# Seven products instead of eight for two column blocks of the gating's v, in a two-layer hybrid decoder step

## Chip, cores and metric

The kernel runs on one core of a Trainium2 chip. The metric is the device time of one execution in microseconds (us); less is better. All arithmetic is 32-bit floating point; the large matmuls run in the replicated form fp32r, in which each operand is split into a high and a low part and three of the four part products are added (high x high, high x low, low x high).

## What is computed

A trunk of two layers is run for a prompt of 1024 positions and for 64 sample rows (8 sequences of 8), with shared weights and model width 1024. Layer 0 mixes positions by windowed attention, layer 1 by a gating MLP; each is followed by a convolutional feed-forward block. The change lies in the gating of layer 1:

```python
def sgu_mix(h, w_in, b_in, ln_g, ln_b, w_sp, b_sp, w_out):
    z = jax.nn.gelu(h @ w_in + b_in)
    u, v = jnp.split(z, 2, axis=-1)          # 2048 columns each
    v = layernorm(v, ln_g, ln_b)
    ...
    mixed = jnp.einsum('gts,bnsgc->bntgc', wm, vb) + b_sp[:, :tc].T[None, None, :, :, None]
    out = (u * mixed.reshape(B, T, D_SGU)) @ w_out
    return out, v
```

Here h is the normed input (1088 rows of 1024). The layer norm of v runs over all 2048 columns, so v is computed first; the spatial mixing runs over chunks of 128 positions.

## The kernel before

Most matrix products of the kernel go by a scheme of seven products (Strassen's in Winograd's form): rows, inner dimension and columns are each halved, and seven products of sums of the blocks replace eight products of the blocks. The function `pair` (L1659) does it for two tiles of 128 output columns at a time, with weights made by `pair_weights` (L1612), and sums of the blocks of h made by the norm (`Norm7.sums`, L1369, and `Norm7.split`, L1382, which splits them into high and low parts `th` and `tl`). The u half of the gating already goes this way.

The v half does not. It is computed with positions on the partitions: the stationary operand is a 128x128 block of h (transposed, high or low part), the moving operand is a row block of weights, 128x512. The loop over `n` (L1977) takes four blocks of 512 columns. For each there are nine row tiles: eight of the prompt (24 matmuls each: 8 inner blocks x 3 part products) and one of the samples, which has high and low parts side by side in one tile of 128 (`norm.pair`) and so takes 16. That makes 208 matmuls of 512 columns a block. The last three tiles of a block are done inner block by inner block (VLAST), so that the four weight buffers come free one after the other. Each tile is then finished: VectorE adds the bias (L2016), ScalarE applies GELU (L2019), VectorE takes statistics for the layer norm (L2020), and a DMA on ScalarE's queue writes the tile to a scratch in memory (L2022), from where it is later read column by column for the mixing (`sgu_load`).

Around this, in the order of the program:
- During n=0 the norm that precedes the stage is finished (`norm.finish`, L1405 and `apply`): VectorE and ScalarE write the second half of the columns of the operands `ha` and `hb`.
- During n=0, after the fourth tile, the spatial weights are loaded on SP's queue (`load_spatial`, L1948), and after the ninth tile masked on GpSimd and summed by one matmul (`prep_spatial`, L1961).
- During n=1 to n=3, after every second tile, GpSimd makes one of eight sums of blocks of h (`norm.sums`), and ScalarE and VectorE split it, all for the u half behind.
- At the end of n=3 the first weights for u are prepared, then `ln_stats` closes the layer norm's statistics, and the u loop begins.

Weights come in one stream (`Stream`, class at L262) of units of 128x1024, in the order of `plan()`, loaded on SP's queue into two raw buffers; `split` casts the high part on ScalarE and subtracts for the low part on VectorE, into a pool of eight weight buffers. Working tiles come from one pool of 37 slots of 128x1106 (NSLOT, L28); PSUM has eight banks. The order of instructions on each engine in this part is chosen by the compiler's list scheduler: by place in the program (moved up by `high_priority`) and by when, by its own model, operands and buffers are ready; at run time each engine takes its queue in that order.

Of the kernel before, what the change touches and what calls it, by code (L numbers as in the profile page):

```python
# [10 lines left out]
F32 = mybir.dt.float32  # L11
# [15 lines left out]
SG_BLOCKS = [4, 4, 4, 4]  # L27
NSLOT = 37  # L28
VLAST = 3
FRA, FRB = 1, 2  # L30
CHF = ((0, 416), (416, 416), (832, 256))
FIN = ((0, 2, 1), (2, 4, 0), (4, 6, 1), (6, 8, 0))
# [35 lines left out]
def plan():  # L68

    u = []  # L70
    for e in START:
        if e[0] == "A":
            u += [(("adaq", e[1], e[2]), 1024)]
        elif e[0] == "S":
            u += [(("ada", 0, SH1, e[1]), 1024)]
        elif e[0] == "W":
            u += [(("qkv", 2, e[1]), 1024)]
    for n in (0, 1):
        u += [(("qkv", n, kp), 1024) for kp in range(4)]
# [24 lines left out]
    for n in range(4):  # L104
        u += [(("sguv", n, kp), 1024) for kp in range(4)]
    for j in range(0, NS, 2):
        u += [(("ua", 2, j), 1024), (("ub", 2, j), 1024)]
    u += down("w_sgu_out", SG_BLOCKS)
    u += ffn(1)
    return u  # L110


def lay_weights(inp):
# [30 lines left out]
    for key, _ in plan():  # L144
# [3 lines left out]
        elif k == "adaq":  # L148
            a = ada[0][key[2] * 512:key[2] * 512 + 512, 1024 + key[1] * 256:1280 + key[1] * 256]
            a = a.reshape(4, 128, 256).transpose(1, 0, 2)  # L150
        elif k == "qkv":
            a = kpair(wq, key[1], key[2])
        elif k == "sguv":
            a = kpair(sin[:, DSGU:], key[1], key[2])
        elif k == "up":
# [105 lines left out]
class Stream:  # L261
# [11 lines left out]
    def dma(s):  # L273
# [15 lines left out]
    def split(s):  # L289
# [48 lines left out]
HP = 200  # L338


def build(nc, tc, a, ctx):
# [941 lines left out]
    class Norm7:  # L1283
# [82 lines left out]

            return s.ab[k][h][:, part, :]

        def sums(s, z, q, e):  # L1369

            zc = slice(z * 272, z * 272 + 272)
            a0, a1, b0, b1 = (s.ab[2 * q + b][h][:, :, zc].bitcast(F32) for b in range(2) for h in range(2))
            t = slot([128, 4, 272], name="T")
            for i, (p, m) in enumerate(((a1, a0), (b1, a1))):
                e.tensor_sub(t[:, 2:4, :], p, m)
                e.tensor_add(t[:, i, :], t[:, 2, :], t[:, 3, :])
            for i, (p, m) in ((2, (b1, 0)), (3, (b0, 2))):
                e.tensor_sub(t[:, i, :], p[:, 0, :], t[:, m, :])
                e.tensor_add(t[:, i, :], t[:, i, :], p[:, 1, :])
            s.tt[z, q] = t  # L1380

        def split(s, z, q):  # L1382
            t = s.tt.pop((z, q))
            s.th[z, q], s.tl[z, q] = slot([128, 4, 272], F32R, name="th"), slot([128, 4, 272], F32R, name="tl")
            A.copy(s.th[z, q], t)
            V.tensor_sub(s.tl[z, q], t, s.th[z, q].bitcast(F32))

        def rhs(s, i, z, q, part):

            if i < 4:  # L1390
                k, h = ((2 * q, 0), (2 * q + 1, 0), (2 * q + 1, 1))[i - 1]
                return s.half(k, h, part)[:, z * 272:z * 272 + 272]
            return (s.tl if part else s.th)[z, q][:, {5: 0, 7: 1, 6: 2, 4: 3}[i], :]

        def drop(s, what):

# [578 lines left out]
    todo = [(z, q) for z in range(2) for q in range(4)]  # L1975
    taken = []
    for n in range(4):  # L1977
        bv = slot([128, 512], name="bv")
        SP.dma_start(bv, a["bv"][0:1, n * 512:n * 512 + 512].broadcast_to([128, 512]))
        ws.ahead(4)  # L1980
        un = [ws.take("sguv") for _ in range(4)]
        ps = {}
# [16 lines left out]
        for i, t in enumerate((0, 1, 4, 5, 2, 3, 6, 7, 8)):  # L1999
            M = 128 if t < 8 else 64  # L2000
            if i <= 9 - VLAST:
                for kp in range(4):
                    for t_ in ((t,) if i < 9 - VLAST else (2, 3, 6, 7, 8)[5 - VLAST:]):
                        v_mm(t_, kp)
                    if i == 9 - VLAST:
                        un[kp] = None
                        if n < 3:
                            with tc.high_priority(offset=HP):
                                ws.split()
                        elif kp == 0:  # L2010
                            gen = pair_weights()
                            W = next(gen)
                        else:
                            next(gen)
            v = slot([128, 512], name="v")
            V.tensor_add(v[:M], ps[t][:M], bv[:M])  # L2016
            if M == 64:
                V.tensor_add(v[:M], ps[t][64:128], v[:M])
            A.activation(v[:M], v[:M], AF.Gelu_apprx_tanh)  # L2019
            V.bn_stats(stats[:M, t, n, :], v[:M])  # L2020
            if t < 8:
                A.dma_start(vscr[n, :, :, t, :], v.rearrange("p (j c) -> p j c", c=128))  # L2022
            else:
                A.dma_start(vscs[:, n * 512:n * 512 + 512], v[:64])
# [17 lines left out]
    del norm.pair  # L2042
    for k in range(0, 8, 2):
        norm.ab[k][1] = None
    for _ in range(4):
        next(gen)
    for t in range(9):
        ln_stats(t)

# [113 lines left out]
```

## Time and profile before

| what | value |
|---|---|
| median of 3 runs | 2590.87 us (2586.61 to 2592.92) |
| profiled execution, its own time | 2589.49 us |
| its span, first to last instruction | 2587.7 us |
| mean granted TensorE clock | 0.994 |
| HBM read, written | 228.06 MB, 63.07 MB |

The names of the engines in the profile: PE is TensorE's matmul, PEld its weight load, DVE is VectorE, ACT is ScalarE, POOL is GpSimd, SP is SyncE, whose queue issues the loads. L375 is the helper through which every matmul goes, so matmuls are told apart by the tile that they write: `v` in the stage that is changed, `m` in the pairs of seven products, `acc` and `misc` elsewhere. A row of a group has: line, engine, operation, output<-inputs, shapes, count | busy us, mean ns of one | idle us of the engine before them, and who ended it. A row of a stretch has, for each engine, busy us and the number of instructions.

### The profile page before, as it was taken

How to read it: one execution, taken by the hardware profiler on the slowest of the kernel's cores; microseconds unless marked ns; L12 is line 12 of the kernel's file. 1: busy time of each engine (PE TensorE's matmuls, PEld its weight loads, DVE VectorE, ACT ScalarE, POOL GpSimd, SP SyncE). 2: the span in 40 equal slices, each digit the busy share in tenths (PEclk: the TensorE clock that was granted, in tenths of full speed). 3: DMA queues.
4: the chain of work that ended last, by engine and by line, in shares of the span. 5: the costliest groups of instructions: out<-in, count | busy, mean ns of one | idle time of the engine just before them, and what ended most of it. 6: DMA issues, size and time to landing. Idle time of an engine off the chain costs nothing.

```text
span 2587.7 us, 45783 instructions
## 1 busy us (share of the span) xinstructions
PE 2535.6 (98%) x17916; PEld 2373.8 (92%) x17916; DVE 1616.8 (62%) x3254; ACT 982.6 (38%) x1939; POOL 1240.9 (48%) x1392
## 2 busy tenths in 40 slices
PE   7999999999999999999999999999999999999998
PEld 4667789999999999999788999999999999999998
DVE  5416866767767764456744555655687766676545
ACT  3216854533334331114325655212553333332203
POOL 2325631399999900001643755212179999940003
PEclk9999999999999999999999999999999999999999
DMA  8342214022222275453322534522112222254211
GB/s 302 102 153 100 74 57 139 10 80 81 85 81 76 93 288 181 159 187 127 91 84 76 169 127 156 200 99 74 66 59 76 76 80 79 77 192 158 89 45 70
DMA packets 113943, 292.20 MB, mean 113 GB/s; under 512 B 15328, under 2 KB 47136, under 8 KB 113696
## 3 DMA queue, kind: packets, MB, share of 16 engines
q1 hardware_dynamic: 82016, 232.49, 27.4%
q10 hardware_dynamic: 31712, 56.79, 5.8%
q8 instruction: 142, 2.33, 0.4%
q14 instruction: 73, 0.60, 0.1%
HBM read 228.06 MB, written 63.07 MB: 113 GB/s over the span
## 4 chain that ended last, share of the span: by engine, by line
PE 86%; DVE 6%; ACT 3%; POOL 2%; DMA 2%; issue 1%; SPq 0%; ACTq 0%; DVEq 0%; POOLq 0%
PE m L375 32%; PE acc L375 23%; PE misc L375 9%; PE v L375 7%; PE y L375 5%; PE u L375 5%; PE adaps L375 1%; POOL w L1622 1%; DMA raw<-wts 1%; ACT P L841 1%; PE rs L375 1%; DVE cv L1823 1%; PE pv L375 1%; DVE cv L1810 1%; PE sc L375 1%
## 5 line engine op out<-in xcount | busy, mean ns | idle before, releaser
L375 PE MATMUL m<-th,w 128*128 128x272 f32 x2944 | 562.6, 288 | 6.4 <-DVE ext L1676 6.3
L375 PEld LDWEIGHTS m<-th,w 128*128 128x128 f32 x2944 | 466.2, 188 | 7.0 <-issue 6.6
L375 PE MATMUL m<-tl,w 128*128 128x272 f32 x1472 | 424.9, 289 | 0.0
L536 DVE SCALAR_TENSOR_TENSOR x<-acc,mod,x 128x384 f32<-128x384 f32 (+1 forms) x312 | 159.6, 567 | 237.6 <-PE acc L375 232.0
L375 PE MATMUL m<-hb,w 128*128 128x272 f32 x2208 | 294.3, 289 | 0.0
L375 PEld LDWEIGHTS m<-hb,w 128*128 128x128 f32 x2208 | 285.1, 190 | 0.0
L375 PEld LDWEIGHTS m<-tl,w 128*128 128x128 f32 x1472 | 277.5, 189 | 0.0
L375 PE MATMUL acc<-gh,whi 128*128 128x384 f32 (+1 forms) x1152 | 255.9, 330 | 1.1 <-DVE mixed L2089 0.8
L375 PE MATMUL acc<-gl,whi 128*128 128x384 f32 (+1 forms) x1152 | 253.6, 328 | 0.6 <-DVE gl L1729 0.6
L375 PE MATMUL acc<-gh,wlo 128*128 128x384 f32 (+1 forms) x1152 | 253.2, 327 | 0.0
L309 ACT CAST whi<-raw 128x1024 fp32r<-128x1024 f32 (+1 forms) x108 | 109.7, 1017 | 377.9 <-PE acc L375 230.5
L1622 POOL TENSOR_TENSOR w<-raw,w 128x512 fp32r<-128x512 f32 x138 | 194.5, 1422 | 82.2 <-ACT w L1621 76.0
L375 PEld LDWEIGHTS acc<-gh,whi 128*128 128x128 f32 x1152 | 194.7, 188 | 10.2 <-issue 6.2
L375 PEld LDWEIGHTS acc<-gl,whi 128*128 128x128 f32 x1152 | 195.6, 188 | 0.9 <-DVE gl L1729 0.9
L1808 DVE SCALAR_TENSOR_TENSOR cv<-ext,cst,cv 128x1104 f32<-128x1104 f32 x88 | 125.4, 1460 | 112.9 <-ACT cv L1807 53.9
L375 PEld LDWEIGHTS acc<-gh,wlo 128*128 128x128 f32 x1152 | 195.7, 188 | 0.0
L1621 ACT CAST w<-Sa 128x512 fp32r<-128x512 f32 x92 | 56.8, 622 | 307.9 <-POOL Sa L1632 162.0
L1676 DVE TENSOR_TENSOR ext<-ev,m 128x272 f32<-128x272 f32 (+1 forms) x456 | 137.5, 338 | 47.6 <-PE m L375 39.3
L1303 POOL TENSOR_TENSOR nsq<-nsq 128x544 f32<-128x544 f32 x18 | 24.9, 1385 | 273.4 <-ACT nsq L1296 273.4
L1810 DVE SCALAR_TENSOR_TENSOR cv<-ext,cst,cv 128x1104 f32<-128x1104 f32 x88 | 155.6, 1802 | 0.1
L375 PE MATMUL m<-ha,w 128*128 128x272 f32 x1104 | 146.6, 289 | 0.0
L375 PEld LDWEIGHTS m<-ha,w 128*128 128x128 f32 x1104 | 141.2, 188 | 0.6
(293 smaller groups left out, 5506.8 us busy)
## 6 DMA issues: line engine op xcount, KB each, us to landing
raw<-wts SPq DMA_DIRECT2D x238, 512.0 KB, 4.0
wada<-wts SPq DMA_DIRECT2D x54, 512.0 KB, 4.3
pscr<-cv ACTq DMA_DIRECT2D x44, 544.0 KB, 5.5
p<-pscr SPq DMA_DIRECT2D x40, 544.0 KB, 5.5
xscr<-x ACTq DMA_DIRECT2D x24, 512.0 KB, 2.8
x<-xscr SPq DMA_DIRECT2D x24, 512.0 KB, 8.3
sscr<-mixed ACTq DMA_DIRECT2D x16, 544.0 KB, 3.5
vscr<-v ACTq DMA_DIRECT2D x32, 256.0 KB, 2.6
```

What stands on the lines that cost most here:

```text
L309: nc.scalar.copy(hi[:, :c], r[:, :c])
L375: PE.matmul(out, lhsT=l, rhs=r, start=start, stop=stop)
L536: V.scalar_tensor_tensor(xv, p[:, 0:w], gp, xv, op0=ALU.mult, op1=ALU.add)
L841: A.activation(p, p, AF.Exp, bias=nm[:, h:h + 1], scale=0.125, accum_out=su[:, h:h + 1])
L1303: (V if z or m == 7 else G).tensor_add(s.ss[z], s.ss[z], q)
L1621: A.copy(t[:, 0:512], src)
L1622: eng.tensor_sub(t[:, 512:1024], src, t[:, 0:512].bitcast(F32))
L1676: V.tensor_add(o, f(p), f(q))
L1808: V.scalar_tensor_tensor(t[:, 0:1104], e[:, 1:1105], cw(jj * 3 + 1), t[:, 0:1104], op0=ALU.mult, op1=ALU.add)
L1810: V.scalar_tensor_tensor(t[:, 0:1104], e[:, 0:1104], cw(jj * 3), t[:, 0:1104], op0=ALU.mult, op1=ALU.add)
L1823: V.tensor_mul(tg[:, 0:SEQ], tg[:, 0:SEQ], tu[:, 0:SEQ])
```

## The change

Blocks n=0 and n=1 stay as they are. Blocks n=2 and n=3 (`VW`) go by seven products. The rows are halved into positions 0 to 511 and 512 to 1023, the inner dimension by the parity of its 128-blocks, and the 512 columns into two of 256. The stationary operands are the block sums of h which the u half needs anyway; they are now made over all 544 columns of a half at once (four of them, in tiles of twice the length) and during n=0 and n=1, one of them on VectorE. The weight sums for v are new: `v_weights` makes eight pairs of high and low tiles, with GpSimd for sums and low parts. Each product has two halves z of two row tiles, in one bank of 2 x 256 columns, and VectorE adds the products up on the way out. The sample rows do not take the scheme: they use four plain quarters of the weights, of which one (index 0) serves only them. The spatial weights are loaded and prepared behind the last block.

The stream's units of these blocks are now quarters of 256 columns; every second one is loaded into a slot instead of a raw buffer. The core of the diff (`v_done` is the old finishing of a tile as a function; the sums over 544 columns and the changed indices of the u half are left out):

```diff
@@ plan(), dma(), split()
-        u += [(("sguv", n, kp), 1024) for kp in range(4)]
+        u += [(("vq" if n in VW else "sguv", n, kp), 1024) for kp in range(4)]
...
-        if i < s.NFIRST or (key[0] == "ada" and key[1] == 0 and key[2] != G2):
+        if i < s.NFIRST or key[0] == "vq" and key[2] % 2 or (key[0] == "ada" and key[1] == 0 and key[2] != G2):
             t = s.first()
...
-        if key[0] in ("ada", "adaq", "ua", "ub"):
+        if key[0] in ("ada", "adaq", "ua", "ub", "vq"):
...
+    def v_weights():
+        W = {}
+        def parts(i, src):
+            W[i] = [wp.tile([128, 1024], F32R, name="v7", tag="w") for _ in range(2)]
+            A.copy(W[i][0], src)
+            G.tensor_sub(W[i][1], src, W[i][0].bitcast(F32))
+        yield W
+        r11 = ws.take("vq")[1]
+        parts(1, r11)
+        yield
+        r12 = ws.take("vq")[1]
+        parts(2, r12)
+        yield
+        r22 = ws.take("vq")[1]
+        parts(4, r22)
+        yield
+        r21 = ws.take("vq")[1]
+        parts(0, r21)
+        G.tensor_add(r22, r21, r22)
+        yield
+        G.tensor_sub(r21, r11, r21)
+        G.tensor_sub(r11, r22, r11)
+        parts(6, r11)
+        yield
+        G.tensor_sub(r12, r12, r11)
+        parts(5, r22)
+        yield
+        parts(7, r21)
+        yield
+        parts(3, r12)
+        yield
+
+    def v_pair(n, W, bv, prep):
+        ev, bk, vt = {}, {}, {}
+        sps = bank("v")
+        def mul(i, z):
+            p = bk[i, z] = bank("v").rearrange("p (g c) -> p g c", c=256)
+            for g_ in range(2):
+                c = slice((2 * z + g_) * 128, (2 * z + g_) * 128 + 128)
+                m = 0
+                for q in range(4):
+                    for xl, wl in ((0, 0), (0, 1), (1, 0)):
+                        mm(p[:, g_, :], norm.cols(i, q, xl)[:, c], W[i][wl][:, q * 256:q * 256 + 256], m == 0, m == 11)
+                        m += 1
+            return p
+        def sample(i):
+            f, b = ((1, 0), (0, 0), (0, 1), None, (1, 1))[i]
+            for q in range(4):
+                for wl in range(2):
+                    mm(sps[:, f * 256:f * 256 + 256], norm.pair[:, 2 * q + b, :], W[i][wl][:, q * 256:q * 256 + 256],
+                       i in (1, 4) and q + wl == 0, i in (2, 0) and q + wl == 4)
...
+        for i in (1, 2, 4, 6, 5, 7, 3):
+            if i == 1:
+                e0 = slot([128, 2, 2, 256], name="ve")
+                e1 = slot([128, 2, 2, 256], name="ve")
+            for z in range(2):
+                p = mul(i, z)
+                a = e0[:, z]
+                if i == 1:
+                    V.tensor_add(a, p, wide(bv[:, 0:256]))
+                elif i == 2:
+                    V.tensor_add(out(0, 0, z), a, p)
+                elif i == 6:
+                    V.tensor_add(a, a, p)
+                elif i == 5:
+                    V.tensor_add(e1[:, z], a, p)
+                    V.tensor_add(a, a, wide(bv[:, 512:768]))
+                elif i == 7:
+                    V.tensor_add(a, a, p)
+                    V.tensor_add(out(1, 0, z), a, bk.pop((4, z)))
+                    done(0, z)
+                    V.tensor_add(out(1, 1, z), a, bk.pop((5, z)))
+                elif i == 3:
+                    V.tensor_add(out(0, 1, z), e1[:, z], p)
+                    done(1, z)
...
+            if i in (1, 2, 4):
+                sample(i)
+            W.pop(i)
+            prep()
+            if i == 4:
+                sample(0)
+                W.pop(0)
...
@@ the loop over n, now n = 0 and 1 only
-            if n == 0 and i == 3:
-                wsp, wbd, rb, tri = load_spatial()
-            if n == 0 and i == 8:
-                prep_spatial(wsp, wbd, rb, tri)
-                del tri
-            if n and i % 2 == 1:
-                while taken:
-                    norm.split(*taken.pop(0))
-                if todo:
-                    norm.sums(*todo[0], G)
-                    taken.append(todo.pop(0))
+            if n == 0 and i == 7:
+                norm.sums(0, G)
+            if n == 1 and i in (1, 3, 5):
+                norm.split(i // 2)
+                norm.sums(i // 2 + 1, V if i == 1 else G)
...
+    norm.split(3)
+    for n in VW:
+        bv = load_bias(n)
...
+        v_pair(n, W, bv, prep)
...
     for _ in range(4):
         next(gen)
+    wsp, wbd, rb, tri = load_spatial()
+    prep_spatial(wsp, wbd, rb, tri)
```

`done(h, z)` applies GELU to two row tiles at once and then finishes each as before. `prep` makes the next pair of weight tiles, of this block or of the one behind it.

More of the change, by code (lines that the diff above doesn't have):

```diff
@@ L29 @@
 VLAST = 3
+VW = (2, 3)
 FRA, FRB = 1, 2
@@ L1367, in half, with sums, split, cols @@
             return s.ab[k][h][:, part, :]
[L1369 to L1373, printed above, removed]
+        def sums(s, q, e):
+            a0, a1, b0, b1 = (s.ab[2 * q + b][h].bitcast(F32) for b in range(2) for h in range(2))
+            t, t2 = s.tt[q] = [slot([128, 2, 544], name="T") for _ in range(2)]
             for i, (p, m) in enumerate(((a1, a0), (b1, a1))):
[L1375 to L1388, printed above, removed]
+                e.tensor_sub(t2, p, m)
+                e.tensor_add(t[:, i, :], t2[:, 0, :], t2[:, 1, :])
+            for i, p, m in ((0, b1, t), (1, b0, t2)):
+                e.tensor_sub(t2[:, i, :], p[:, 0, :], m[:, 0, :])
+                e.tensor_add(t2[:, i, :], t2[:, i, :], p[:, 1, :])
+        def split(s, q):
+            for j, t in enumerate(s.tt.pop(q)):
+                hi = s.th[q, j] = slot([128, 2, 544], F32R, name="th")
+                lo = s.tl[q, j] = slot([128, 2, 544], F32R, name="tl")
+                A.copy(hi, t)
+                V.tensor_sub(lo, t, hi.bitcast(F32))
+        def cols(s, i, q, part):
             if i < 4:
                 k, h = ((2 * q, 0), (2 * q + 1, 0), (2 * q + 1, 1))[i - 1]
-                return s.half(k, h, part)[:, z * 272:z * 272 + 272]
-            return (s.tl if part else s.th)[z, q][:, {5: 0, 7: 1, 6: 2, 4: 3}[i], :]
+                return s.half(k, h, part)
+            j = {5: 0, 7: 1, 6: 2, 4: 3}[i]
+            return (s.tl if part else s.th)[q, j // 2][:, j % 2, :]
+        def rhs(s, i, z, q, part):
+            return s.cols(i, q, part)[:, z * 272:z * 272 + 272]
         def drop(s, what):
@@ L1973, in ln_stats, with v_done @@
         V.scalar_tensor_tensor(mv[:M, t, 0:1], mv[:M, t, 0:1], -1.0, mv[:M, t, 1:2], op0=ALU.mult, op1=ALU.mult)
[L1975 to L1979, printed above, removed]
+    def v_done(v, t, n):
+        M = 128 if t < 8 else 64
+        V.bn_stats(stats[:M, t, n, :], v[:M])
+        if t < 8:
+            A.dma_start(vscr[n, :, :, t, :], v.rearrange("p (j c) -> p j c", c=128))
+        else:
+            A.dma_start(vscs[:, n * 512:n * 512 + 512], v[:64])
@@ new lines, in v_weights @@
+    def v_weights():
[23 more added lines that the diff above has]
+        G.tensor_sub(r12, r12, r11)
+        del r11
+        parts(5, r22)
+        del r22
+        yield
+        parts(7, r21)
+        del r21
+        yield
+        parts(3, r12)
+        del r12
+        yield
@@ L1980, in build, with load_bias @@
+    def load_bias(n):
+        bv = slot([128, 768], name="bv")
+        SP.dma_start(bv[:, 0:512], a["bv"][0:1, n * 512:n * 512 + 512].broadcast_to([128, 512]))
+        if n in VW:
+            V.tensor_sub(bv[:, 512:768], bv[:, 256:512], bv[:, 0:256])
+        return bv
+    for n in range(min(VW)):
+        bv = load_bias(n)
         ws.ahead(4)
@@ L2006, in build @@
                         un[kp] = None
-                        if n < 3:
+                        if n + 1 < min(VW):
                             with tc.high_priority(offset=HP):
@@ L2010, in build @@
                         elif kp == 0:
-                            gen = pair_weights()
+                            gen = v_weights()
                             W = next(gen)
                         else:
-                            next(gen)
+                            with tc.high_priority(offset=HP):
+                                next(gen)
             v = slot([128, 512], name="v")
-            V.tensor_add(v[:M], ps[t][:M], bv[:M])
+            V.tensor_add(v[:M], ps[t][:M], bv[:M, 0:512])
             if M == 64:
@@ L2019, in build @@
             A.activation(v[:M], v[:M], AF.Gelu_apprx_tanh)
[L2020 to L2024, printed above, removed]
+            v_done(v, t, n)
             del v, ps[t]
@@ L2029, in build, with prep @@
                 norm.finish()
-            if n == 0 and i == 3:
-                wsp, wbd, rb, tri = load_spatial()
-            if n == 0 and i == 8:
-                prep_spatial(wsp, wbd, rb, tri)
-                del tri
-            if n and i % 2 == 1:
-                while taken:
-                    norm.split(*taken.pop(0))
-                if todo:
-                    norm.sums(*todo[0], G)
-                    taken.append(todo.pop(0))
+            if n == 0 and i == 7:
[3 more added lines that the diff above has]
+                norm.sums(i // 2 + 1, V if i == 1 else G)
         del bv, un
-    del norm.pair
     for k in range(0, 8, 2):
         norm.ab[k][1] = None
+    norm.split(3)
+    for n in VW:
+        bv = load_bias(n)
+        more = []
+        def prep():
+            for _ in gen:
+                return
+            if not more:
+                more.append(v_weights() if n < 3 else pair_weights())
+                more.append(next(more[0]))
+            next(more[0])
+        v_pair(n, W, bv, prep)
+        gen, W = more
+        del bv
     for _ in range(4):
         next(gen)
+    wsp, wbd, rb, tri = load_spatial()
+    prep_spatial(wsp, wbd, rb, tri)
+    del tri
+    del norm.pair
     for t in range(9):
```

26 lines of the change are left out of this document (added).

## Prediction

> **What bounds the kernel now.** I read the page first: busy time and the chain of work that ended last.
>
> ```profile
> span 2587.7 us, 45783 instructions
> PE 2535.6 (98%) x17916; PEld 2373.8 (92%) x17916; DVE 1616.8 (62%) x3254; ACT 982.6 (38%) x1939; POOL 1240.9 (48%) x1392
> PE 86%; DVE 6%; ACT 3%; POOL 2%; DMA 2%; issue 1%; SPq 0%; ACTq 0%; DVEq 0%; POOLq 0%
> ```
>
> TensorE is busy 98% of the span and carries 86% of the chain. A share of the span is a mean over stages, so I read next the chain in order of time, for the stage that is changed and its neighbours (start us, us, what).
>
> ```profile
> 1246.69 1.91 DVE hb L1363 x2
> ...
> 1260.44 15.61 PE v L375 x66
> 1276.05 0.86 PE misc L375 x2
> 1276.90 145.14 PE v L375 x624
> 1422.05 21.05 PE m L375 x168
> 1443.09 4.49 PE acc L375 x36
> 1447.58 2.45 PE m L375 x18
> ```
>
> Column blocks n=1, 2 and 3 of v are one piece of 145.14 us with 624 matmuls, so 208 a block, and the products of u follow with no gap. What TensorE saves here moves everything behind it forward, as long as nothing else comes late. The busy time by stage (n=0, then the three blocks, then the first pair of u) shows how much room the others have.
>
> ```profile
> core 0: us, PE busy (x) PEld busy (x) DVE busy (x) ACT busy (x) POOL busy (x), PEclk, DMA share, GB/s
> 1217.90:1276.90 59.00, 53.91 (x237) 41.63 (x236) 48.90 (x94) 25.67 (x64) 28.22 (x24) 1.00 0.33 96
> 1276.90:1325.28 48.38, 48.38 (x210) 39.10 (x209) 20.60 (x26) 12.90 (x17) 21.81 (x20) 1.00 0.31 95
> 1325.28:1373.66 48.38, 48.38 (x209) 39.06 (x208) 22.11 (x28) 13.96 (x18) 15.82 (x16) 1.00 0.31 96
> 1373.66:1422.04 48.38, 48.38 (x210) 39.06 (x210) 20.12 (x40) 27.68 (x36) 18.80 (x17) 1.00 0.25 72
> 1422.05:1443.10 21.05, 21.05 (x170) 21.05 (x170) 10.03 (x30) 13.88 (x32) 17.25 (x18) 1.00 0.59 186
> ```
>
> In n=2 and n=3 TensorE is busy the whole 48.38 us at a granted clock of 1.00; VectorE and GpSimd are under half. Only n=0 has TensorE idle: 59.00 - 53.91 = 5.1 us.
>
> **TensorE's work.** A 512-column matmul of the stage costs 48.38 / 208 = 0.2326 us. The new ones have 256 columns. The trace has such a stream, with a new stationary operand for each matmul, in the last projection:
>
> ```profile
> 2571.15 0.39 PE L375 MATMUL misc<-gh,wlo 128*128 128x256 f32 x1
> 2571.38 0.28 PE L375 MATMUL misc<-gh,whi 128*128 128x256 f32 x1
> 2577.68 0.28 PE L375 MATMUL misc<-gh,wlo 128*128 128x256 f32 x1
> 2571.38:2577.68 6.30, 6.30 (x54) 6.30 (x54) 2.18 (x8) 0.00 (x0) 1.00 0.35 127
> ```
>
> The 54 include the one begun at 2571.15, so 53 starts in 6.30 us: 0.1189 us each, weight loads hidden (both columns 6.30). By the diff a block takes 7 products x 2 halves x 2 groups x 12 = 336 matmuls, and the sample rows 4 x 8 = 32: 368 of 256 columns in place of 208 of 512. That is 368 x 0.1189 = 43.75 us for 48.38; twice, 87.5 for 96.8: **-9.2 us**. The dearest bound is the pace of the 272-column pairs, 21.05 / 168 = 0.1253 us: 46.1 a block, -4.5 in all. I take 0.1189, a row of exactly this width.
>
> [...]
>
> **The other engines inside n=2 and n=3.** The prices:
>
> ```profile
> L316 POOL TENSOR_TENSOR wlo<-raw,whi 128x1024 fp32r<-128x1024 f32 x3 | 7.7, 2567 | 2.2 <-PE m L375 2.2
> L309 ACT CAST whi<-raw 128x1024 fp32r<-128x1024 f32 x9 | 9.4, 1050 | 18.9 <-PE v L375 18.3 <-ACT v L2019 0.6
> L2016 DVE TENSOR_TENSOR v<-v,bv 128x512 f32<-128x512 f32 x24 | 16.5, 689 | 46.3 <-PE v L375 39.2 <-DMA bv<-bv 3.8 <-DMA vscr<-v 3.1
> L2020 DVE BATCH_NORM_STATS2 stats<-v 128x6 f32<-128x512 f32 x23 | 15.7, 690 | 12.7 <-ACT v L2019 12.7
> L2019 ACT ACTIVATE v<-v 128x512 f32<-128x512 f32 x25 | 15.6, 631 | 49.8 <-DVE v L2016 49.7
> L1385 ACT CAST th<-T 128x1088 fp32r<-128x1088 f32 x8 | 8.8, 1100 | 3.1 <-ACT v L2019 1.8 <-POOL T L1375 0.7 <-POOL T L1378 0.6
> L1386 DVE TENSOR_TENSOR tl<-T,th x8: 1280/1283/1303, 1299.9 to 1390.9; 128x1088 fp32r<-128x1088 f32 x8
> raw<-wts SPq DMA_DIRECT2D x238, 512.0 KB, 4.0
> vscr<-v ACTq DMA_DIRECT2D x32, 256.0 KB, 2.6
> ```
>
> GpSimd: each block has 8 splits and 4 sums of weights, 12 operations of 1024 columns: 12 x 2.57 = 30.8 us of 43.75. VectorE: 20 additions and 9 statistics of 512 columns, 29 x 0.69 = 20 us. ScalarE: 8 casts of 1.05, 4 GELUs at the 1.10 of a 1088-column pass and one of 0.63: 13.4 us. All fit beside TensorE, so the question is order. The tightest chain is product 6. TensorE wants it after products 1, 2, 4 and the four sample parts: 3 x 48 + 32 = 176 matmuls, 20.9 us. In n=2, GpSimd has from the block's start the split of W0, the sum, two differences and the split of W6, five operations: 12.8 us, and a cast of 1.05, 13.9 in all: 7 us to spare. Products 5, 7 and 3 come 5.7 us apart and need one or two operations each. VectorE's longest knot is product 7, 6 additions and 4 statistics, 6.9 us against 5.7 of TensorE; the eight banks hold more than a further product, so TensorE does not see it. A slot (37, all spoken for in this stage) can come late by an output's store, 2.6 us after GELU and statistics; the same banks cover that, and without them it would be 2.6 us a block. The new odd weight quarters use slots too, with the same bytes and 4.0 us to land, and are fetched a block ahead. SP is in order: a load that waits for a slot holds the bias load behind it, which VectorE waited for before as well (3.8 us) while TensorE stood nowhere. Cost on the path: 0.
>
> **n=0 and n=1.** n=0 ends on VectorE, which finishes the norm while TensorE waits the 5.1 us. GpSimd interferes there:
>
> ```profile
> 1243.23 0.28 DVE L1363 TENSOR_TENSOR ha<-nts,ha 128x32 fp32r<-128x32 f32 x2
> 1246.13 1.74 POOL L1962 TENSOR_TENSOR wsb<-wsb,tri 128x512 f32<-128x512 f32 x1 [3.47 <-DMA tri<-tri]
> 1247.83 0.72 POOL L1963 TENSOR_TENSOR wsb<-wsb,tri 64x256 f32<-64x256 f32 x1
> 1252.56 1.47 POOL L1375 TENSOR_TENSOR T<-ha 128x544 f32<-128x544 f32 x1 [4.01 <-ACT hb L1358]
> L1375 POOL TENSOR_TENSOR T<-ha x8: 1357/1364/2276, 1252.6 to 1374.7; 128x544 f32<-128x544 f32 x8
> ```
>
> Two 128x32 writes took 0.28 us at 1243.23 and 1.91 in the chain at 1246.69, beside the spatial weight's product of 1.74. The change takes that product and its 0.72 us neighbour out of n=0, and sums(0) comes in a block earlier in the program: two operations of 1088 and six of 544 columns, 2 x 2.73 + 6 x 1.36 = 13.6 us. Before, GpSimd had 2.5 of spatial work and 7.9 of sums (1252.56 to 1260.44) in that stretch, 10.4 at most. If the sums start as soon as the first rows are normed, the difference, 13.6 - 10.4 = 3.2 us, is the most that can fall on the path; if they start where they did, 1.6 us (1.91 - 0.28) are won. I take 0 between the two. The sums that VectorE makes in n=1 (2 x 1.28 + 6 x 0.64 = 6.4 us) lie beside 48.38 us with 20.6 busy.
>
> **The step into u.** The spatial weights are now loaded and multiplied behind the last block. The matmul on them (0.86 us, only moved) stands in TensorE's order ahead of u's products, and these wait if it waits: for a load, and the products of 1.74 and 0.72. Nothing excludes 0; the dear end is 4.0 + 2.5 = 6.5 us. I take **+1.0**, near the cheap end, because the loads have no input and can go as soon as a slot is free, and the row of the same matmul at 1276.05 shows no wait. The layer norm's nine square roots come at the end together; the first use of u's gate is 21.05 us into u, which covers them.
>
> **Sum.** -9.2 + 0 + 1.0 = -8.2. The profiled execution took 2589.49 us (span 2587.7 and 1.8 around it), so 2581.3; the median of the three runs is 2590.87, 1.4 above, which gives **2582.7**. A measurement of this kernel tells about 0.3%, 7.8 us: faster is under 2583.1.
>
> **Rivals.**
>
> A, the forecast, alone 2579 to 2586 (from n=0's gain of 1.6 and the runs' spread of some 2 on the low side to 3 us at the step into u): 0.60, of which 0.45 falls below 2583.1.
>
> B, sums lock VectorE out in n=0: the dear end, +3.2: 2585.9, the same. For it: the 1.91 at 1246.69; three slots that spatial work held are free for it. Against: a T tile waited for a slot until 1252.56. 0.17. [...]
>
> C, slower: GpSimd becomes the bound of n=2 and n=3.
>
> ```profile
> L1629 POOL TENSOR_TENSOR Sa<-raw x46: 1277/2412/2447, 515.8 to 2272.8; 128x512 f32<-128x512 f32 x46
> L1629 POOL TENSOR_TENSOR Sa<-raw 128x512 f32<-128x512 f32 x7 | 9.0, 1289 | 0.6 <-DMA raw<-wts 0.6
> ```
>
> The same 512-column sum takes 1.28 us at best and 2.41 in the median of the whole run. At 2 x 2.41 = 4.82 us an operation, a block needs 12 x 4.82 = 57.8 us, 14.1 above TensorE's 43.75; both, +28, less 8: some 2611. It binds from 43.75 / 12 = 3.65 us an operation and eats the gain at 4.0. Against it: in the u stage, where VectorE is as busy as here, the mean is 1.289 (second row), and most of VectorE's additions here read PSUM. 0.16, with weaker forms down to 2591.
>
> D, the pace is not reached: 256 columns at 0.1253: -4.5 + 1.0, so 2587.4, the same. 0.07.
>
> **Numbers.** Faster 0.45 (A's part); same 0.15 + 0.17 + 0.07 = 0.39; slower 0.16. The range, 2578 to 2594, holds A, B, D and the mildest of C, and leaves out most of C and a little below.
>
> **What would show it.** Matmuls v at 0.119 us apart, no TensorE idle in 87.5 us for n=2 and n=3, GpSimd's 1024-column operations near 2.6 us. Wrong if weight loads v wait for a split (C), if n=0 has more than 5.1 us idle (B), or if TensorE stands at the first misc matmul before u.

## The result, and the profile after

The changed kernel takes 2603.32 us (median of 5 runs, 2602.03 to 2608.7) beside 2592.03 (5 runs, 2586.61 to 2594.43): the ratio is 1.0052, with an interval of 1.0037 to 1.0067. It is 11 us slower; 2582.7 was forecast, in a range of 2578 to 2594. The profiled execution took 2602.13 us.

The page has the same three lines as before:

```profile
span 2600.3 us, 46453 instructions
PE 2537.1 (98%) x18236; PEld 2391.4 (92%) x18236; DVE 1639.4 (63%) x3276; ACT 976.0 (38%) x1929; POOL 1276.4 (49%) x1376
PE 86%; DVE 5%; ACT 3%; POOL 2%; DMA 2%; issue 1%; SPq 0%; ACTq 0%; DVEq 0%; POOLq 0%
```

They look like those of before: TensorE 98% busy, 86% of the chain. Nothing in these lines shows the loss. The busy time by stage does: n=0; n=1; n=2 and n=3 up to their last matmul; the stretch from there to u's first matmul; u's first pair.

```profile
core 0: us, PE busy (x) PEld busy (x) DVE busy (x) ACT busy (x) POOL busy (x), PEclk, DMA share, GB/s
1217.83:1281.21 63.38, 55.86 (x235) 42.84 (x234) 52.33 (x93) 25.52 (x63) 17.82 (x10) 0.92 0.28 85
1281.21:1329.61 48.40, 48.40 (x210) 39.08 (x209) 31.62 (x35) 16.10 (x20) 30.10 (x16) 1.00 0.27 85
1329.61:1420.72 91.11, 88.66 (x737) 88.33 (x735) 47.72 (x69) 30.00 (x33) 71.21 (x39) 0.98 0.32 94
1420.72:1429.20 8.48, 1.17 (x4) 0.57 (x3) 3.86 (x11) 4.19 (x6) 4.90 (x5) 0.75 0.98 284
1429.20:1451.87 22.67, 22.67 (x171) 22.15 (x170) 11.42 (x32) 13.45 (x35) 15.82 (x13) 0.94 0.31 110
```

The five make 234.04 us, where the same work took 225.2 before (1217.90 to 1443.10). By stage: n=0 and n=1, 111.78 for 107.38; n=2 and n=3, 91.11 for 96.76; a stretch of 8.48 that was not there; the first pair, 22.67 for 21.05. That is +4.40 - 5.65 + 8.48 + 1.62 = +8.85. The rest of the span is 3.8 us longer; it comes up again below.

The chain in order of time names who holds TensorE. First n=0, then product 6 of n=2, then the step into u (L380 is here what L375 was; L1999 is the split for a low part in `v_weights`, L1970 the masking):

```profile
1246.59 2.59 DVE hb L1368 x2
1249.82 4.08 DVE hb L1364 x2
1262.45 55.94 PE v L380 x239
...
1350.66 2.37 POOL v L1999
1353.08 62.08 PE v L380 x511
```

```profile
1417.71 6.42 DMA vscr<-v
1424.20 2.43 DMA tri<-tri
1426.79 1.28 POOL wsb L1970
1428.11 2.08 PE misc L380 x2
1430.19 21.84 PE m L380 x168
```

Each of these three waits carries a second cost, which the column PEclk shows. In three stretches of this stage TensorE ran at half clock; in the kernel before, every stretch of it stood at 1.00.

```profile
1251.00:1261.00 10.00, 6.97 (x14) 4.14 (x14) 10.00 (x10) 0.88 (x2) 9.53 (x7) 0.50 0.00 0
1353.50:1356.50 3.00, 3.00 (x16) 3.00 (x15) 0.00 (x0) 0.00 (x0) 3.00 (x2) 0.50 0.87 231
1425.50:1431.50 6.00, 3.39 (x9) 2.36 (x10) 2.54 (x2) 3.86 (x12) 4.71 (x5) 0.50 0.98 283
```

The products themselves run as forecast, 48 matmuls in 5.83 us, 0.12 us each:

```profile
1414.98 5.83 PE L380 MATMUL v<-v,hb 128*128 128x256 f32 x48
```

So the theory: the seven products bring what was said, and three waits for other engines, with half a clock behind each, take more. The rival theory: one of the three is the loss, and the others are noise or would be hidden without it. In every experiment the kernel before ran on the same chip; its medians there were 2587.4 to 2588.5.

### The profile page after: what moved, and what is told of

It reads as the page before. It is cut to its first block, busy times and chain, and to the rows that moved or that the text cites. A ratio compares the mean times of both kernels' runs of the same rounds, so it can differ in the third digit from the quotient of the medians.

```text
span 2600.3 us, 46453 instructions
## 1 busy us (share of the span) xinstructions
PE 2537.1 (98%) x18236; PEld 2391.4 (92%) x18236; DVE 1639.4 (63%) x3276; ACT 976.0 (38%) x1929; POOL 1276.4 (49%) x1376
## 4 chain that ended last, share of the span: by engine, by line
PE 86%; DVE 5%; ACT 3%; POOL 2%; DMA 2%; issue 1%; SPq 0%; ACTq 0%; DVEq 0%; POOLq 0%
PE m L380 34%; PE acc L380 23%; PE misc L380 9%; PE y L380 6%; PE v L380 5%; PE u L380 5%; PE adaps L380 1%; ACT P L846 1%; PE rs L380 1%; DMA raw<-wts 1%; DVE cv L1831 1%; PE pv L380 1%; DVE cv L1818 1%; PE sc L380 0%; DVE cv L1816 0%
## 5 line engine op out<-in xcount | busy, mean ns | idle before, releaser
L380 PE MATMUL m<-th,w 128*128 128x272 f32 x2944 | 563.6, 288 | 7.5 <-DVE ext L1684 7.5
L380 PEld LDWEIGHTS m<-th,w 128*128 128x128 f32 x2944 | 465.9, 189 | 8.2 <-issue 7.6
L380 PE MATMUL m<-tl,w 128*128 128x272 f32 x1472 | 424.8, 289 | 0.0
L380 PE MATMUL m<-hb,w 128*128 128x272 f32 x2208 | 292.3, 288 | 0.0
L380 PEld LDWEIGHTS m<-hb,w 128*128 128x128 f32 x2208 | 283.2, 189 | 0.0
L380 PEld LDWEIGHTS m<-tl,w 128*128 128x128 f32 x1472 | 277.3, 188 | 0.0
L380 PE MATMUL acc<-gh,whi 128*128 128x384 f32 (+1 forms) x1152 | 256.4, 330 | 1.1 <-DVE mixed L2238 0.9
L380 PE MATMUL acc<-gl,whi 128*128 128x384 f32 (+1 forms) x1152 | 253.5, 328 | 0.6 <-DVE gl L1737 0.6
L380 PE MATMUL acc<-gh,wlo 128*128 128x384 f32 (+1 forms) x1152 | 253.8, 328 | 0.0
L314 ACT CAST whi<-raw 128x1024 fp32r<-128x1024 f32 (+1 forms) x100 | 101.3, 1014 | 365.2 <-PE acc L380 232.6
L380 PEld LDWEIGHTS acc<-gh,whi 128*128 128x128 f32 x1152 | 195.0, 188 | 10.0 <-issue 5.8
L380 PEld LDWEIGHTS acc<-gl,whi 128*128 128x128 f32 x1152 | 195.8, 188 | 0.9 <-DVE gl L1737 0.9
L380 PEld LDWEIGHTS acc<-gh,wlo 128*128 128x128 f32 x1152 | 196.0, 188 | 0.0
L380 PE MATMUL m<-ha,w 128*128 128x272 f32 x1104 | 148.5, 290 | 0.0
L380 PEld LDWEIGHTS m<-ha,w 128*128 128x128 f32 x1104 | 142.5, 189 | 1.5 <-ACT mv L1979 0.5
```

The source lines that it names most:

```text
L314: nc.scalar.copy(hi[:, :c], r[:, :c])
L380: PE.matmul(out, lhsT=l, rhs=r, start=start, stop=stop)
```

## The experiments

### The moved step alone, in the kernel before

```diff
-            if n == 0 and i == 3:
-                wsp, wbd, rb, tri = load_spatial()
-            if n == 0 and i == 8:
-                prep_spatial(wsp, wbd, rb, tri)
...
     for _ in range(4):
         next(gen)
+    wsp, wbd, rb, tri = load_spatial()
+    prep_spatial(wsp, wbd, rb, tri)
...
```

> The kernel before with only the move of the spatial weights behind the last block of v; nothing goes by seven products there. Theory (the step is late because the tiles of two rows of v and the stored outputs hold the slots, so it belongs to both parts): with fewer slots held, 2 to 5 us between the last v and the first m matmul, of which n=0 gives back up to 1.6 as GpSimd's masking is gone from it; total within 4 us of before. Rival (the place in the program alone makes it): 7 us or more at the step, total 5 to 9 us above before.

Measured: 2606.55 us, ratio 1.0068 (1.0054 to 1.0081). This one move, with eight products throughout, costs at least as much as the whole change (1.0052). The rival is right about the step; the loss, some 18 us by the ratio, is more than either said. At the step:

```profile
1430.77 2.07 PE L375 MATMUL misc<-wsb,ones 128*128 128x512 f32 x2 [9.87 <-POOL wsb L1962]
1426.00:1436.00 10.00, 5.23 (x17) 4.20 (x18) 0.96 (x7) 4.46 (x14) 5.79 (x10) 0.50 0.55 186
```

TensorE waits 9.87 us for the masking, then runs at half clock. From n=2's first matmul to u's first, the profile has 107.92 us for 96.8, and the first pair has 23.41 for 21.05. n=0 got no shorter in return (61.72 us up to the first matmul of n=1, for 58.44), though the masking had left it. GpSimd's sums began 30.50 us into the stage (1244.32), while the norm was being finished, some 4 us earlier than before (34.66 us, 1252.56). TensorE's idle in n=0 is 5.75 us for 5.1, but it also ran at half clock in two stretches of some 3.4 us, which the kernel before has not:

```profile
1251.80:1255.10 3.30, 2.87 (x7) 2.29 (x8) 3.30 (x5) 0.00 (x0) 3.14 (x4) 0.50 0.02 5
```

### The step behind u's first pair

The changed kernel, with loading and masking given out behind the products of the first u pair:

```diff
-    wsp, wbd, rb, tri = load_spatial()
-    prep_spatial(wsp, wbd, rb, tri)
...
         W = W1
+        if j == 0:
+            wsp, wbd, rb, tri = load_spatial()
+            prep_spatial(wsp, wbd, rb, tri)
...
```

> The spatial weights' loads, masking and matmul are moved behind the products of the first u pair; all else is the changed kernel. Theory (three places, each with its own price): the step into u, 8.5 us between the last v matmul and the first m matmul, goes, and with it the half clock in the first pair (21.84 us and a late acc instead of 21.05); some 9 us of the changed kernel's time, so about 2594 (before plus 1 to 3). Rival (the 37 slots are all taken, so the wait only moves to another tile): a new gap of similar length near the start of u, gain under 3 us, 2600 or more.

Measured: 2601.3 us, ratio 1.0048 (1.0035 to 1.0062); the change had 1.0052. The rival is right: the gap ahead of u is gone, but the wait went into the pair, which takes 30.4 us in place of 22.67:

```profile
1437.62 0.60 PE L380 MATMUL m<-th,w 128*128 128x272 f32 x1 [2.64 <-ACT ev L1695]
1452.20 1.13 PE L380 MATMUL misc<-wsb,ones 128*128 128x512 f32 x2 [2.49 <-POOL wsb L1970]
```

The masking waits for its loads here too, and ScalarE now comes late to evict the first product. Moving the step as a whole does not settle it; the runs below go on to its loads and to ScalarE's queue.

### A gate for the sums in n=0

Before the first sums, GpSimd copies one column of the last block that the norm writes, and the sums are queued behind that copy:

```diff
+    gate = c4.tile([128, 1], F32, name="gate")
...
             if n == 0 and i == 7:
-                norm.sums(0, G)
+                late = G.tensor_copy(gate, norm.ab[7][1][:, 1, 543:544].bitcast(F32))
+                with tc.issue_after(late.ins):
+                    norm.sums(0, G)
```

> GpSimd's first block sum waits, by a one-column copy of the last operand that the norm writes, until the norm is done; all else is the changed kernel. Theory (GpSimd's long sums lock VectorE out while it finishes the norm, and TensorE's idle then halves its clock): the two-input writes of VectorE at 1246 to 1262 run at 0.1 to 0.45 us again, TensorE's idle in n=0 falls from 7.2 to at most the 4.8 of before, no half clock in n=0, n=0 shorter by 5 to 7 us, total near 2597. Rival (VectorE is simply later there, through the scheduler's order): n=0 unchanged within 1 us, and the later sums make the weights of product 6 later, so 2603 or more.

Measured: 2587.91 us, ratio 1.0006 (0.9994 to 1.0018), where the change had 1.0052: 12 us less, from one copy of 0.59 us. n=0 falls from 63.38 to 52.05 us, by 11.3 where 5 to 7 were expected, with TensorE idle 0.28, and PEclk is 1.00. The other two waits stay as they were (2.44 us for product 6, 7.48 at the step), so the loss in n=0 hides neither. First the changed kernel's GpSimd and VectorE, then the same operations with the gate:

```profile
1245.94 3.09 POOL L1379 TENSOR_TENSOR T<-ha 128x1088 f32<-128x1088 f32 x1 [3.38 <-DVE ha L1364]
1246.52 2.66 DVE L1368 TENSOR_TENSOR hb<-nts,hb 128x32 fp32r<-128x32 f32 x2
1249.74 4.16 DVE L1364 SCALAR_TENSOR_TENSOR hb<-nt,mod,hb 128x240 fp32r<-128x240 f32 x2
1251.08 2.55 POOL L1379 TENSOR_TENSOR T<-hb,ha 128x1088 f32<-128x1088 f32 x1
```

```profile
1242.16 0.28 DVE L1368 TENSOR_TENSOR hb<-nts,hb 128x32 fp32r<-128x32 f32 x2
1243.00 0.84 DVE L1364 SCALAR_TENSOR_TENSOR hb<-nt,mod,hb 128x240 fp32r<-128x240 f32 x2
1248.88 0.59 POOL L2169 COPY gate<-hb 128x1 f32<-128x1 f32 x1 [10.67 <-DVE hb L1368]
1249.42 2.80 POOL L1379 TENSOR_TENSOR T<-ha 128x1088 f32<-128x1088 f32 x1
```

Two writes of 128x32 take 0.28 us alone and 2.66 us beside the sum; they end 0.15 us after it (1249.18 and 1249.03). The pair of 240 columns takes 0.84 us alone and 4.16 beside the sums that follow, and ends 0.27 us after the second of them (1253.90 and 1253.63). In these rows VectorE's short operations end just behind GpSimd's long ones. With the gate, VectorE's last pair, which comes behind the copied column, still takes 3.15 us beside the first sum (from 1249.34), but TensorE does not wait for it.

### The same gate in the kernel before

```diff
+    gate = c4.tile([128, 1], F32, name="gate")
...
+            if n == 0 and i == 7:
+                late = G.tensor_copy(gate, norm.ab[7][1][:, 1, 543:544].bitcast(F32))
             if n == 0 and i == 8:
-                prep_spatial(wsp, wbd, rb, tri)
+                with tc.issue_after(late.ins):
+                    prep_spatial(wsp, wbd, rb, tri)
...
-                    norm.sums(*todo[0], G)
+                    with tc.issue_after(late.ins):
+                        norm.sums(*todo[0], G)
```

> The kernel before, with GpSimd's long operations of n=0 (the masking of the spatial weights and the norm's sums) held until the last norm block is finished. Theory (GpSimd's long two-input operations stretch VectorE's finish of the norm, and TensorE waits for that, in the kernel before too): n=0 falls from 58.4 to about 52 us, and the kernel stands 5 to 7 us under the one before, near 2581. Rival (what the gate gained in the changed kernel was the cost of the changed sums alone): n=0 stays at 58, the time within 2 us of the one before; or the spatial weights' product, which now comes after the gate, holds TensorE by 2 to 3 us and leaves 3 to 4 of the gain.

Measured: 2583.34 us, ratio 0.9983 (0.9973 to 0.9993). n=0 falls from 58.44 to 52.52 us, as expected; the time falls by 4, a little under the 5 to 7 expected. So the kernel before lost some 6 us of n=0 in the same way. The stage, in the same pieces (n=0, n=1, the two blocks, the first pair), is the one against which the products are to be judged:

```profile
1221.87:1274.39 52.52, 52.24 (x237) 41.54 (x235) 42.98 (x93) 25.45 (x64) 19.22 (x16) 1.00 0.36 109
1274.39:1323.13 48.74, 48.74 (x210) 39.23 (x209) 20.59 (x27) 12.88 (x17) 30.01 (x30) 1.00 0.30 92
1323.13:1419.93 96.80, 96.80 (x417) 78.16 (x416) 42.46 (x67) 41.68 (x53) 34.38 (x34) 1.00 0.28 84
1419.93:1440.98 21.05, 21.05 (x170) 21.04 (x168) 10.03 (x30) 14.07 (x32) 17.42 (x18) 1.00 0.59 186
```

### The fourth sums on VectorE

```diff
-                norm.sums(i // 2 + 1, V if i == 1 else G)
+                norm.sums(i // 2 + 1, V if i in (1, 5) else G)
```

> The fourth block sum is made on VectorE instead of GpSimd; all else is the changed kernel. Theory (GpSimd reaches the tail of n=1 with that sum undone, so the chain for product 6 starts some 9 us late): GpSimd has no sum after 1303, the wait of product 6 (2.4 us) and the half clock behind it go, the two blocks n=2 and n=3 take 87.5 to 88 us instead of 91.1; total near 2599.5. Rival (the chain of five GpSimd operations and a cast is itself too long): the wait stays at 1 us or more.

Measured: 2599.82 us, ratio 1.0044 (1.0031 to 1.0056). In n=2 the wait ahead of product 6 falls from 2.45 to 1.63 us, and the clock stays at 1.00 there. GpSimd's order in the changed kernel shows where the 2.45 came from:

```profile
1340.67 2.60 POOL L1999 TENSOR_TENSOR v<-raw,v 128x1024 fp32r<-128x1024 f32 x1
...
1348.30 2.40 POOL L2018 TENSOR_TENSOR raw<-raw,raw 128x1024 f32<-128x1024 f32 x1
1350.66 4.69 POOL L1999 TENSOR_TENSOR v<-raw,v 128x1024 fp32r<-128x1024 f32 x2
```

The split of W0 (the weights of index 0) begins at 1340.67, 11 us into n=2 (1329.61), since the fourth sums had kept GpSimd until 1334.9 and a split and a sum came behind them; and L2018, which is for product 3, the last, stands ahead of W6's split at 1350.66. In this run the sums have left GpSimd, and a wait of 1.63 us stays for another reason: VectorE, which makes the sums now, comes late with the bias of n=1's last tiles, ScalarE's GELU waits for that, W0's cast stands behind the GELU, and GpSimd waits for the cast:

```profile
1332.71 0.63 ACT L2159 ACTIVATE v<-v 128x512 f32<-128x512 f32 x1 [7.77 <-DVE v L2156]
1336.59 2.89 POOL L1999 TENSOR_TENSOR v<-raw,v 128x1024 fp32r<-128x1024 f32 x1 [5.86 <-ACT v L1998]
```

So the rival's number came (1 us or more), but its cause is not seen: GpSimd stands idle for 5.86 us ahead of the chain.

### The gate, and the triangles in the slot of the spatial weights

```diff
-        wsb = slot([128, 768], name="wsb")
+        wsb = slot([128, 960], name="wsb")
...
+        tri = wsb[:, 768:960]
+        SP.dma_start(tri[:, 0:128], a["tri"])
+        SP.dma_start(tri[0:64, 128:192], a["tri_s"])
         rb = slot([128, 2, 4, 128], name="rb")
...
-        tri = slot([128, 192], name="tri")
...
```

> The changed kernel with the sums of n=0 gated and with the triangles loaded into the slot of the spatial weights, ahead of the bias rows. Theory (the step into u waits for the triangles' load alone, which stood behind the bias rows' wait for a slot): the wait of 7.5 us ahead of the spatial weights' product goes, and with it the half clock of the first pair; 8 to 9 us less than with the gate alone, 2579 against 2588. Rival (the same moved wait as with the masking behind the first pair: slots or evictions hold TensorE for some 2.5 us at a later place, with its own half clock): 2583 to 2586.

Measured: 2586.61 us, ratio 0.9996 (0.9987 to 1.0004): by the ratios some 2.6 us less than the gate alone, not 8 to 9. The wait for the masking is 4.75 us in place of 7.48. SP's queue shows what is left:

```profile
1404.86 1.70 SPq L291 DMA_DIRECT2D raw<-wts  x2
1406.61 0.57 SPq L1963 DMA_DIRECT2D wsb<-tri  x1
```

Two weight loads stand ahead of the triangles and wait until 1404.86 for raw buffers. The triangles go at 1406.61 and take 5.6 us to land, and the masking ends only ahead of 1413.74, where TensorE goes on. Neither theory of this run had that right: it was not the slot alone, but the whole queue ahead of a load that comes last.

### The last product's difference behind product 6's split

The run with gate and triangles, and:

```diff
-            G.tensor_sub(W[i][1], src, W[i][0].bitcast(F32))
+            return G.tensor_sub(W[i][1], src, W[i][0].bitcast(F32))
...
-        parts(6, r11)
+        low = parts(6, r11)
         yield
-        G.tensor_sub(r12, r12, r11)
+        with tc.issue_after(low.ins):
+            G.tensor_sub(r12, r12, r11)
```

> As the run with gate and triangles, and in the chain of the weights' combinations the difference for the last product is issued behind the split for product 6. Theory (product 6 waits for GpSimd's chain, in which that difference of 2.3 us stands ahead of the split): the wait of 2.4 us in n=2 and the 3.4 us at half clock behind it go, 3 to 4 us less, near 2575. Rival (the splits are late because the fourth sums fill GpSimd in the tail of n=1, and the order behind them hardly matters): a wait of 1 to 2 us stays and the time falls by under 1.5 us.

Measured: 2582.09 us, ratio 0.9978 (0.9968 to 0.9988), 4.5 us less than without the edit. By the profiles, though, the two blocks up to u took only 1.6 us less (93.81 for 95.39); the wait for W6 is 1.19 us for 2.44. The stage agrees with the rival, the time rather with the theory; runs of one kernel spread by 5 to 9 us here, so I go by the stage. Where the rest of the 4.5 us comes from stays open.

### The same, with the fourth sums on VectorE

The edit of the run with VectorE's sums, on top of the last.

> As the run with gate, triangles and the moved difference, and the fourth sums on VectorE instead of GpSimd. Theory: no wait above 0.5 us for GpSimd is left in n=2 and n=3, which take the products' own time and no more, some 91 us; 2574 to 2575. With the kernel before and its gate near 2581, the seven products are then worth 6 to 8 us, against the 8.2 of the prediction. Rival (VectorE has no room there, and ScalarE's casts wait behind GELUs that wait for VectorE): 1 to 2 us slower than the run without this edit, with waits for ScalarE's casts at product 0 or 6.

Measured: 2583.49 us, ratio 0.9979 (0.9971 to 0.9988). The wait for W6 falls to 0.39 us, as expected; the time is that of the run without the edit, where 2574 to 2575 were expected. What still stands is the step: 4.45 us for the masking, and 23.02 us for the first pair. With it the changed kernel is no faster than the gated kernel before (0.9983), though its profile has the stage, from the first v matmul to the first `acc`, at 216.06 us for 219.11.

### The spatial weights held from n=0, in two slots

The last run's edits without a late step: loading, masking and the sum go back into n=0, behind the gate, so that weights and bias rows keep two slots through n=2 and n=3.

```diff
+            if n == 0 and i == 3:
+                wsp, wbd, rb, tri = load_spatial()
...
                 with tc.issue_after(late.ins):
                     norm.sums(0, G)
+                    prep_spatial(wsp, wbd, rb, tri)
...
-    wsp, wbd, rb, tri = load_spatial()
-    prep_spatial(wsp, wbd, rb, tri)
```

> The changed kernel with the gate, the moved difference and the fourth sums on VectorE, and the spatial weights loaded, masked and summed in n=0 as in the kernel before, behind the gate, so that they hold two slots through n=2 and n=3. Theory (the three waits took the products' gain, and nothing else does): the step into u has no wait, the first pair 21.05 us, n=2 and n=3 some 88 to 90 us; first v product to first acc some 212 us against 219 of the gated kernel before, the time near 2577. Rival (the two slots are what the products need: their evictions and stores wait for slots): waits of 2 us and more inside n=2 and n=3, n=2 to the first u product over 93 us, the time at or above 2582.

Measured: 2583.67 us, ratio 0.9986 (0.9973 to 0.9998). The step's wait is gone. The time is the rival's, the stage is neither's: from n=2 to the first u product it takes 92.16 us, where the theory had 88 to 90 and the rival over 93. n=2 has waits of 1.65 us (for `tl`, a split of a sum) and 1.76 (for product 6), n=3 one of 1.33, all under the rival's 2 us, and ScalarE's eviction holds the first pair by 4.07. The pair takes 27.70 us.

### One slot: the masked weights held, the rest behind

```diff
     def prep_spatial(wsp, wbd, rb, tri):
...
+    def spatial_sum(wsp):
+        rb = slot([128, 2, 4, 128], name="rb")
+        SP.dma_start(rb[:, 1].rearrange("p g t -> p (g t)"), a["bsp"].broadcast_to([128, 512]))
+        ps = misc()
+        mm(ps, ones, wsp.rearrange("p g t -> p (g t)"), True, True)
+        A.copy(rb[:, 0].rearrange("p g t -> p (g t)"), ps)
+        return rb
...
+    rb = spatial_sum(wsp)
     del norm.pair
```

> As the run that holds two slots, but only the masked weights are held from n=0 (one slot); the bias rows and the sum over the weights stay behind the products. Theory: TensorE's wait at the step is gone as well, since the product needs the masked weights alone; within 1 us of the run that holds two. Rival (slots decide): 2 us or more faster than the run that holds two, since it leaves one slot more to the products.

Measured: 2575.82 us, ratio 0.9961 (0.9948 to 0.9974): faster than the kernel before and the changed one, and by 8 us than the run with two slots, as the rival said; the stage is shorter by 5.3 (215.78 us for 221.11). The edit also moves the bias rows' load, the sum and its copy, so that it is the slot alone is not shown; that the seven products can run beside one held slot is. What is left is the eviction in the first pair:

```profile
1423.60 0.39 PE L380 MATMUL m<-th,w 128*128 128x272 f32 x1 [3.18 <-ACT ev L1695]
1416.38 0.58 ACT L1976 COPY rb<-misc 128x512 f32<-128x512 f32 x1
1416.98 1.28 ACT L1982 ACT_TABLE_LOAD   x1
1418.28 0.85 ACT L1982 ACTIVATE mv<-mv 128x1 f32<-128x1 f32 x8
1419.04 1.87 ACT L2224 ACTIVATE vj<-vj,mv 128x128 f32<-128x128 f32 x4
1421.63 1.65 ACT L2224 ACTIVATE vj<-vj,mv 128x128 f32<-128x128 f32 x4 [0.73 <-DVE mv L1984]
1423.19 0.64 ACT L1695 COPY ev<-m 128x272 f32<-128x272 f32 x2
```

ScalarE has the copy of the sum, a table load, eight square roots and eight normalizations queued ahead of the eviction `ev`, 6.8 us of it.

### The eviction first

```diff
-    rb = spatial_sum(wsp)
-    for t in range(9):
-        ln_stats(t)
...
+    def first():
+        nonlocal rb
+        if rb is None:
+            rb = spatial_sum(wsp)
+            for t in range(9):
+                ln_stats(t)
+            sgu_load(0)
+            sgu_norm(0)
+            sgu_load(1)
+        next(gen)
...
-            pair(norm, W, place, lambda: next(gen), lambda i: None)
+            pair(norm, W, place, first, lambda i: None)
```

> As the run that holds the masked weights alone, and the sum over them, its copy, the layer-norm statistics and the first normalization are given out behind the first product of the first u pair instead of ahead of it, so that ScalarE evicts that product first. Theory (the 3.2 us wait for the eviction in the first pair comes from ScalarE's queue: copy, table load and normalization ahead of it): the wait goes, the first pair falls from 26.4 to 21 to 22 us, no half clock is left in the stage, the time falls by 4 to 5 us to near 2571. Rival (the wait moves again, to the gate behind the first pair, which needs the normalized block and the bias rows): a new wait of 2 us or more between the first pair and the second, the time within 2 us of 2576.

Measured: 2574.6 us (2573.63 to 2577.59), ratio 0.9948 (0.9934 to 0.9961): 14 us under the kernel before. The stage is as the theory said; the time fell by less, 3.4 us by the ratios for 4 to 5, and the two intervals overlap. In the stage one wait above 0.25 us is left, 1.48 for product 6 in n=2 (GpSimd waits 7.38 us there for W0's cast, as with the fourth sums on VectorE alone), and no half clock:

```profile
1220.31:1272.36 52.05, 51.76 (x235) 41.32 (x234) 42.17 (x93) 25.45 (x63) 18.98 (x12) 1.00 0.36 111
1272.36:1320.76 48.40, 48.40 (x210) 39.08 (x209) 41.95 (x36) 15.35 (x18) 28.73 (x14) 1.00 0.28 85
1320.76:1409.20 88.44, 86.96 (x738) 86.76 (x736) 57.43 (x76) 29.83 (x33) 64.32 (x34) 1.00 0.29 87
1409.20:1431.11 21.91, 21.91 (x173) 21.43 (x172) 14.74 (x43) 13.78 (x34) 13.04 (x11) 1.00 0.53 177
```

Against the gated kernel before, the stage is 210.80 us for 219.11: -8.3, all of it in the third row (88.44 for 96.80). By the ratios it is 0.9948 for 0.9983, some 9 us. That is what the seven products are worth once the waits are gone.

## Why the prediction was wrong

**TensorE's work: right.** 87.5 us were forecast for the two blocks. In the run with the eviction first TensorE is busy 86.96 us there; in the changed kernel 91.11 less the wait of 2.45 and some 1.5 of half clock (16 matmuls from 1353.08 took 3.43 us, 0.214 us each, for 1.90 at 0.1189) leaves 87.1. The 0.1189 us held, not the pairs' 0.1253. Rivals C and D did not come: GpSimd's operations of 1024 columns took 2.4 to 2.7 us, with one of 3.3. That it helps when VectorE's additions read PSUM, which was put against C, was the author's estimate; no run shows it apart.

**The step into u: the costliest failure.** It was priced at +1.0, "because the loads have no input and can go as soon as a slot is free". It cost 8.48 us ahead of u and 1.62 in the first pair, less the 0.86 that its matmul had taken in n=0: 9.2 us, above the dear end of 6.5 too. Three loads into three slots come late one after the other: SP's queue issues them at 1410.99, 1418.46 and 1424.20. The bias rows stand behind a weight load that waits 4.5 us for a raw buffer; the triangles, the last, wait 5.1 us for a slot which a store of v's holds (6.42 us, where the prediction's row had 2.6); the masking needs them, TensorE needs the masking, and u stands behind that matmul. The dear end counted one load and two products; it left out the queue ahead of the load, the slots, and the slow clock behind the wait. The last of these stood in the trace of before, though not in this stage: TensorE waits 3.52 us there ahead of 1988.33, and a stretch at half clock follows.

```profile
1989.20:1992.50 3.30, 3.30 (x16) 3.30 (x16) 2.82 (x10) 1.43 (x3) 3.30 (x5) 0.50 0.23 17
```

The kernel before with this one move came to a ratio of 1.0068; putting the masked weights back into n=0 took the wait away. In the run with one slot a term showed that the prediction had put at nothing: the layer norm's square roots, which u's first pair was to cover, stood with the normalizations ahead of that pair's first eviction, and TensorE waited 3.18 us for it.

**n=0: the second failure.** "I take 0 between the two" was in place of +5.3 us (n=0 and n=1 by +4.40, without the 0.86 that left). Rival B named the sums, beside which VectorE's writes took 2.66 us for 0.28, and had a dear end of 3.2, counted as GpSimd's added time; its sign, more than 5.1 us idle in n=0, came. The argument against it was that the sums had waited for a slot until 1252.56, 34.66 us into the stage; in the changed kernel they began 28.11 us into it (1245.94). The price is not GpSimd's added time. The sums met more of the norm's short operations, two of which took 2.66 us and two 4.16 beside them, for 0.28 and 0.84 alone; of the 5.3 us, 2.4 are idle time (63.38 - 55.86 = 7.5 for 5.1), and the other 2.8 are TensorE's busy time, stretched by half a clock (55.86 for 53.91 - 0.86 = 53.05). The gate shows both. In the kernel before it also shows that 0 had been measured from a floor that was not one: the kernel before was itself 6 us above it.

**The other engines inside n=2 and n=3: the sum right, the order wrong.** "7 us to spare" for product 6 let GpSimd begin the chain at n=2's start with five operations. It still had sums(3) and earlier splits then, and a sixth operation, L2018, stood ahead of the last split. The wait was 2.45 us, with its half clock some 4.0. It is the sign that the prediction gave for rival C, a weight load that waits for a split, without C's cause. A sum of busy times has no order in it.

**Sum.** The three misses are 9.2 - 1.0 = 8.2, 5.3 and about 3.6 us: 17.1. The stage was to gain 8.2 and lost 8.85. The rest of the span, 3.8 us longer, stays open. It lies behind u's first pair, which ended 1148.4 us ahead of the span's end, for 1144.6 before. The kernel before with the move alone has the code of before there and took 1149.5; the last run took 1144.7, and the run with two slots 1141.8. Single executions spread as much: ahead of the stage, where all kernels are alike, the profiles differ by 10 us (1212.0 to 1221.9).

## What to carry to other kernels

When a move frees slots, follow every DMA of the moved step through its queue and its slot, and price the engine behind the last of them; "no input" does not mean "early". Where TensorE waits for VectorE, keep GpSimd's long operations out of that stretch: a one-column copy that reads the last block written did so, and in the changed kernel was worth more (12 us) than the seven products (8 to 9); in the kernel before it was worth 4. Count an idle of TensorE of 3 us as 3 us and, when the clock falls, what its matmuls then lose: some 1.5 us in the stretch of 3.4 behind product 6's wait.

## What the runs showed of the hardware

In the changed kernel the granted clock fell to 0.50 in three stretches of the stage: 10.2 us (1250.9 to 1261.1), 3.4 (1353.3 to 1356.7) and 6.8 (1425.0 to 1431.8). The single idle of 2.45 us that ended at 1353.08 was followed by the second of them, and 3.18 us in the run with one slot by 3.0 us or more (1425.20 to 1428.20). In the longest idles the stretch began while TensorE still waited: behind 7.31 us, 3.7 of the third stretch's 6.8 us were left, and behind 9.87 us, with the move alone, 5.2 of the 10.0 us from 1426 to 1436. Equal idles differ: 2.44 us had such a stretch in the run with the gate (0.50 from 1337.00 to 1340.00), and none in the run with gate and triangles (1.00 from 1342.80 to 1346.20). The single idles of 1.33 to 1.76 us in n=2 and n=3, in the runs with the fourth sums on VectorE, with two slots and with the eviction first, had none. With the move alone, the five idles of n=0, 0.58 to 1.38 us each between 1246.74 and 1258.55, came with two stretches at half clock of some 3.4 us. The four of the kernel before in the same place, 0.76 to 1.42 us each, had none.
